# Two dense feed-forwards: one product of 512 columns in place of two of 256

## The chip, the cores and the metric

The kernel runs on one core of one Trainium2 chip, in one launch, and works on one sequence of 256 tokens with 1024 features. The metric is the device time of a run in microseconds, lower is better. All matrix products are made on TensorE (PE) in a 32-bit format (fp32r) that rounds its operands; the other engines are VectorE (DVE), ScalarE (ACT), GpSimd (POOL) and SyncE (SP), which issues the weight transfers.

## What is computed

The reference is a network of three blocks on the same 256 tokens. Layer 0 has a mixer and a dense feed-forward of width 2816. Layer 1 has another mixer and a mixture of 8 experts of width 3584, of which each token uses 2. A second block has an attention with a convolution beside it, a dense feed-forward of width 2816 and a last norm. The dense feed-forward is this:

```python
def _swiglu(x, w1, w3, w2):
    return (jax.nn.silu(x @ w1) * (x @ w3)) @ w2

# second block, on u = rms_norm(h, ...)
h = h + (jax.nn.silu(u @ w_gate[l]) * (u @ w_up[l])) @ w_down[l]
```

## The kernel before

**Three products for one.** To keep float32 precision, each operand is split into a high part (rounded to fp32r, made by ACT) and a low part (the rest, made by DVE by a subtraction); `mm3` then makes high x high, high x low and low x high and adds all three into one PSUM bank. The low x low product is left out everywhere.

**The weight stream.** All weights lie in memory as blocks of 128 x 2048 floats (1 MB each). `Stream._load` issues their transfers on SP's queue in the order of use, each into a free raw buffer; `_split` makes `wh` on ACT (L102) and `wl` on DVE (L103), each into a free split buffer. A transfer starts when a raw buffer is free, a split when its block has landed and a split buffer has been read to its end by PE. During the experts the raw buffers are those of three pools and one slot more, of the tag `b8` of the pool `xp`; 12 in all.

**A dense feed-forward** (`ffn`) runs over 11 pieces of 256 columns of width. For each it takes one block of w1, one of w3 and one of w2. `proj_cols` makes one projection, transposed: for 2 halves `ct` of 128 columns and 8 pieces `k` of the features, three matmuls of 256 columns (the tokens) with a weight of 128 x 128 each, so 48 matmuls, into the two halves of one PSUM bank. ACT takes Silu of the first projection out of PSUM (L383), DVE multiplies it by the second, still in PSUM (L385), and `parts` splits the product into `ah` and `al`. `out_mms` then makes the product with w2 in matmuls of 512 columns, one piece behind. The first piece (`proj_tok`) is made in another way and is not touched. The first feed-forward stands at about 180 to 367 us of the span, the second at about 1653 to 1835 us.

**Pools and aliases.** The pool `xp` has 6 slots of 8 KB a partition under the tag `b8`. They hold in turn the two parts of the transposed activations (`xTh`, `xTl`), those of a mixer's output (`oTh`, `oTl`), the blocks' outputs (`xn`), and during the experts `xh`, `xl`, `y`, `gy` and one raw weight buffer. Which tile gets which slot follows from the order of allocation and release. A tile that takes a slot waits until the last reader of the tile before has ended.

**The order.** A scheduler of the framework sets, when the program is built, the order in which each engine runs its instructions; each engine then runs strictly in that order and waits where data or a slot is not free. Whatever changes in pools or instructions can so move instructions elsewhere in the program.

**Three places away from the feed-forwards that the prediction speaks of.**

- The start of layer 1 (about 370 to 385 us). The layer norm's output is transposed on PE in groups of 4 (`ptr`, two groups for each 128 tokens: the features 0 to 511, and 512 to 1023) and split into `xTh` and `xTl`; then `proj_tok` multiplies (`pt`). A small weight `w_f`, loaded on POOL's queue, is split on ACT as well (`wfh`).
- The end of layer 1's mixer (about 496 to 528 us): its last products with the output weights read `oTh` and `oTl` (`acc`), then a layer norm for each 128 tokens `tt` (r = input + acc on DVE, L349; a square on ACT, L354, which uses `xn` as scratch; the reciprocal root on POOL; two scalings on DVE, L358 and L359, into `xn`), the router and the first gather for the experts.
- The collection (about 1395 to 1440 us), while the last expert runs: four indirect transfers on POOL's queue fetch rows of the other experts' outputs into the two halves of `gy`, and after each DVE adds them to `y` (L1040). A transfer into a half waits until the addition before it has read that half.

Of the kernel before, what the change touches and what calls it, by code (L numbers as in the profile page):

```python
# [10 lines left out]
F32 = mybir.dt.float32  # L11
F32R = mybir.dt.float32r
# [3 lines left out]
AF = mybir.ActivationFunctionType  # L16
ALU = mybir.AluOpType
AX = mybir.AxisListType

P = 128  # L20
D = 1024
T = 256
# [120 lines left out]
def tile_model(ctx, tc, io, out):  # L143
    nc = tc.nc
    cp = ctx.enter_context(tc.tile_pool(name="cp", bufs=1))
    xp = ctx.enter_context(tc.tile_pool(name="xp", bufs=6))
    rawp = ctx.enter_context(tc.tile_pool(name="rawp", bufs=R_RAW))
    wp = ctx.enter_context(tc.tile_pool(name="wp", bufs=N_SPLIT))
    sp = ctx.enter_context(tc.tile_pool(name="sp", bufs=4))
# [24 lines left out]
    NW = len(moe_order)  # L174
# [4 lines left out]
    ws = Stream(tc, rawp, wp, order, native=[second + i for i in NATIVE2])  # L179
# [5 lines left out]
    def bank(group, name):  # L185

        i = groups[group][turns[group] % len(groups[group])]
        turns[group] += 1
        return ps.tile([P, 512], F32, tag="bank%d" % i, name=name)

    def mmt(name="mm"):
        return bank("mm", name)

    def mm(o, l, r, start, stop):
        nc.tensor.matmul(o, l, r, start=start, stop=stop, skip_group_check=True)  # L195

    def mm3(o, lh, ll, rh, rl, start, stop):
        mm(o, lh, rh, start, False)
        mm(o, lh, rl, False, False)
        mm(o, ll, rh, False, stop)  # L200

    def split_to(oh, ol, src):
        high = nc.scalar.activation(oh, src, AF.Copy)  # L203
        return high, nc.vector.tensor_tensor(ol, src, oh.bitcast(F32), op=ALU.subtract)  # L204

    def tok(tt):
        return slice(tt * P, (tt + 1) * P)
# [50 lines left out]
        return split if full is None else copy_first  # L258

    def new_xT():  # L260
        h = xp.tile([P, 8, T], F32R, tag="b8", name="xTh")
        l = xp.tile([P, 8, T], F32R, tag="b8", name="xTl")
        return h, l

    def new_oT():
        h = xp.tile([P, 8, T], F32R, tag="b8", name="oTh")
# [3 lines left out]
    def take8():  # L270
        return [w if w is None else w.rearrange("p (k n) -> p k n", k=8) for w in ws.take()]

    def take2():
        return [w.rearrange("p (k n) -> p k n", k=2) for w in ws.take()]

    def proj_cols(xT, full=None, group="mm"):

        wh, wl = take8()
        o = bank(group, "pc")
        for ct in range(2):  # L280
            for k in range(8):
                oc = o[:, ct * 256:(ct + 1) * 256]
                if wl is None:
                    mm(oc, wh[:, k, tok(ct)], full[:, k, :], k == 0, k == 7)
                else:
                    mm3(oc, wh[:, k, tok(ct)], wl[:, k, tok(ct)], xT[0][:, k, :], xT[1][:, k, :], k == 0, k == 7)
        return o.rearrange("p (c t) -> p c t", c=2)

    def proj_tok(xT, n=1, group="mm"):

        w_ = [take8() for _ in range(n)]
        o_ = [bank(group, "pt") for _ in range(n)]
        for tt in range(2):
            for (wh, wl), o in zip(w_, o_):
                for k in range(8):
                    mm3(o[:, tt * 256:(tt + 1) * 256], xT[0][:, k, tok(tt)], xT[1][:, k, tok(tt)],
                        wh[:, k, :], wl[:, k, :], k == 0, k == 7)
        o_ = [o.rearrange("p (c t) -> p c t", c=2) for o in o_]
        return o_ if n > 1 else o_[0]
# [18 lines left out]
    def out_mms(acc, oT, w, k0, tt, first, last):  # L318

        for nh in range(2):  # L320
            for kk in range(2):
                mm3(acc[nh], oT[0][:, k0 + kk, tok(tt)], oT[1][:, k0 + kk, tok(tt)],
                    w[0][:, kk, half(nh)], w[1][:, kk, half(nh)], first and kk == 0, last and kk == 1)

    def new_acc(t):
        return [bank("acc%d" % t, "acc%d" % nh) for nh in range(2)]
# [47 lines left out]
    def ffn(fp, fr, fw, xT, n, finish):  # L374

        accs = [new_acc(0), new_acc(1)]
        ws.more(3 * n, (fr, "wraw", 4), late=True)
        ws.wider(3 * n, fw, 1, True)
        ws.first = False

        def gate(shape, h1, h3):
            s1 = fp.tile(shape, F32, tag="s1", name="s1")
            nc.scalar.activation(s1, h1, AF.Silu)  # L383
            a = fp.tile(shape, F32, tag="a", name="a")
            nc.vector.tensor_tensor(a, s1, h3, op=ALU.mult)  # L385
            return a

        def parts(a):
            ah = fp.tile([P, 2, T], F32R, tag="ah", name="ah")
            al = fp.tile([P, 2, T], F32R, tag="al", name="al")  # L390
            split_to(ah, al, a)
            return ah, al


        a = gate([P, 2, 256], *proj_tok(xT, 2))
        for j in range(1, n):
            h1 = proj_cols(xT)
            if j == 1:
                pt = mmt("pa")
                for ft in range(2):  # L400
                    for tt in range(2):
                        nc.tensor.transpose(pt[:, tok(ft * 2 + tt)], a[:, tt, tok(ft)], ident)
                aT = parts(pt.rearrange("p (f t) -> p f t", f=2))
            nxt = parts(gate([P, 2, T], h1, proj_cols(xT)))
            w = take2()
            if j < n - 1:
                for tt in range(2):
                    out_mms(accs[tt], aT, w, 0, tt, j == 1, False)
                aT = nxt
        w1 = take2()  # L410
        for tt in range(2):
            out_mms(accs[tt], aT, w, 0, tt, False, False)
            out_mms(accs[tt], nxt, w1, 0, tt, False, True)
            finish(tt, accs[tt])
# [128 lines left out]
    mrow = cp.tile([P, 1], F32, tag="mrow", name="mrow")  # L543
    nc.gpsimd.memset(mrow, -1.0 / D)
    xT = new_xT()
    for tt in range(2):
        transpose_tile(x[:, tt], "mm", parts_of(xT, tt))
# [7 lines left out]
    with tc.tile_pool(name="l0", bufs=1) as lp:  # L555
# [9 lines left out]
        with tc.tile_pool(name="gla", bufs=1) as gp:  # L565
# [12 lines left out]

            ws.first = True
            misc = proj_cols(xT)  # L580
            kiT = gp.tile([P, T], F32, tag="kiT", name="kiT")
            nc.scalar.activation(kiT, misc[:, 0, :], AF.Copy)
# [5 lines left out]
            for i in range(2):  # L588
                o = proj_cols(xT)
# [11 lines left out]
            for tt in range(2):  # L601
# [3 lines left out]
                for q in range(2):  # L605
# [5 lines left out]
                    for j in range(2):  # L611
                        rl = g2([P, 2, 256], "rl")
                        nc.scalar.activation(rl[:, :, :S], pis[j][:, :, :S], AF.Relu)
                        for i in range(2):
                            h = (2 * q + i) * 2 + j
# [33 lines left out]
            AT, xl = [], []  # L649
            for tt in range(2):  # L650
# [13 lines left out]
                for lv in range(7):  # L664
                    h = 64 >> lv
# [36 lines left out]
            for tt in range(2):  # L702
                po = bank("acc", "pog")
                for h in range(4):
                    a = 2 * (h % 2) + h // 2
# [22 lines left out]
        with tc.tile_pool(name="t0", bufs=1) as tp, tc.tile_pool(name="t0w", bufs=2) as wo:  # L728
# [25 lines left out]
            xT = xT2  # L754
# [3 lines left out]
    with tc.tile_pool(name="f0", bufs=2) as fp, tc.tile_pool(name="f0r", bufs=4) as fr, tc.tile_pool(name="f0w", bufs=1) as fw:  # L758
# [13 lines left out]
        x, xT = xn, xT2  # L772
# [62 lines left out]
    with tc.tile_pool(name="l1", bufs=1) as lp:  # L835
# [75 lines left out]
        with tc.tile_pool(name="t1", bufs=1) as tp, tc.tile_pool(name="t1w", bufs=1) as wo:  # L911
# [27 lines left out]
            def finish(tt, acc):  # L939
                if tt == 1:  # L940
                    transpose_tile(xn[:, 0], "acc0", router(0))
                normed.extend(residual_ln(tp, x, acc, lnp, xn, tt, router(1) if tt else None, 1))
# [22 lines left out]
    with tc.tile_pool(name="moer", bufs=4) as mr, tc.tile_pool(name="moe2", bufs=2) as m2:  # L965
        ws.first = False
        ws.more(NW, (mr, "wraw", 4))
        ws.more(NW, (xp, "b8", 1), late=True)
        xh = xp.tile([P, 2, D], F32R, tag="b8", name="xh")
        xl_ = xp.tile([P, 2, D], F32R, tag="b8", name="xl")  # L970
        y = xp.tile([P, 2, D], F32, tag="b8", name="y")
        for tt in range(2):
            with tc.issue_after((copied[-1] if tt else normed[-2]).ins):
# [59 lines left out]

        def collect():

            gy = xp.tile([P, 2, D], F32, tag="b8", name="gy")
            for tt in range(2):
                for k in range(2):
                    nc.gpsimd.indirect_dma_start(gy[:, k], None, yg_d, bass.IndirectOffsetOnAxis(ap=rg[:, tt, k:k + 1], axis=0))
                    nc.vector.scalar_tensor_tensor(y[:, tt], gy[:, k], gk[:, tt, k:k + 1], y[:, tt], op0=ALU.mult, op1=ALU.add)  # L1040
# [130 lines left out]
        xT = new_xT()  # L1171
# [25 lines left out]
    with tc.tile_pool(name="s1", bufs=1) as lp:  # L1197
# [15 lines left out]
        for ct in range(4):  # L1213
            o = proj_cols(xT, xTf)
# [27 lines left out]
        with tc.tile_pool(name="t2", bufs=1) as tp, tc.tile_pool(name="t2w", bufs=1) as wo:  # L1242
# [3 lines left out]
            xT = new_xT()  # L1246
# [40 lines left out]
    with tc.tile_pool(name="f2", bufs=2) as fp, tc.tile_pool(name="f2r", bufs=4) as fr, tc.tile_pool(name="f2w", bufs=1) as fw:  # L1287
        fing = bcast(fp, io["fin_g"], "fing")

        o = xp.tile([P, 2, D], F32, tag="b8", name="o")  # L1290
# [130 lines left out]
def build(arrays):  # L1421
    import concourse.bacc as _bacc

    nc = _bacc.Bacc("TRN2", target_bir_lowering=False, num_devices=1)
    io = {n: nc.dram_tensor("in_" + n + "_dram", a.shape, mybir.dt.from_np(a.dtype), kind="ExternalInput").ap()
          for n, a in arrays.items()}
    out = nc.dram_tensor("out_0_dram", (T, D), F32, kind="ExternalOutput").ap()
    with tile.TileContext(nc) as tc:
        tile_model(tc, io, out)
    return nc  # L1430
# [9 lines left out]
```

## Time and profile before

| | |
|---|---|
| median of 3 runs | 1846.14 us (1843.38 to 1847.57) |
| the profiled execution, device time | 1845.33 us |
| its span, first to last instruction | 1843.5 us |
| mean granted TensorE clock | 0.982 of full speed |
| PE, DVE, ACT, POOL busy | 97%, 73%, 59%, 5% of the span |
| weight blocks split (wh, wl) | 446 each |
| read from memory | 495.57 MB |

The span leaves out about 1.8 us of the device time at the launch's ends. Busy PE is the share of time in which a matmul was under way; matmuls overlap, so that a busy PE need not be at its peak.

### The profile page before, as it was taken

How to read it: one execution, taken by the hardware profiler on the slowest of the kernel's cores; microseconds unless marked ns; L12 is line 12 of the kernel's file. 1: busy time of each engine (PE TensorE's matmuls, PEld its weight loads, DVE VectorE, ACT ScalarE, POOL GpSimd, SP SyncE). 2: the span in 40 equal slices, each digit the busy share in tenths (PEclk: the TensorE clock that was granted, in tenths of full speed). 3: DMA queues.
4: the chain of work that ended last, by engine and by line, in shares of the span. 5: the costliest groups of instructions: out<-in, count | busy, mean ns of one | idle time of the engine just before them, and what ended most of it. 6: DMA issues, size and time to landing. Idle time of an engine off the chain costs nothing. (4 is left out here: it accounts for less than half of the span.)

```text
span 1843.5 us, 24483 instructions
## 1 busy us (share of the span) xinstructions
PE 1782.0 (97%) x9857; PEld 1512.4 (82%) x9857; DVE 1338.1 (73%) x1363; ACT 1096.1 (59%) x1016; POOL 83.9 (5%) x133
## 2 busy tenths in 40 slices
PE   8999999999999999999999999999998987999998
PEld 7887999888778888888788787887886867889997
DVE  6866544545678888888888888888887877955443
ACT  5454433344567777777777777777775754564442
POOL 1101100010010000000000000000002002000000
PEclk9999999999989999999999999999999998999999
DMA  8442985254379999999999999999998933546530
GB/s 297 161 163 103 390 329 186 89 196 158 117 300 423 381 371 371 382 355 366 374 367 368 381 364 375 371 368 373 366 364 321 361 139 140 206 155 250 190 125 24
DMA packets 75418, 512.50 MB, mean 278 GB/s; under 512 B 8572, under 2 KB 8725, under 8 KB 17312
## 3 DMA queue, kind: packets, MB, share of 16 engines
q1 hardware_dynamic: 66096, 475.62, 68.2%
q0 software_dynamic: 8912, 34.70, 5.0%
q8 instruction: 80, 1.31, 0.3%
q10 hardware_dynamic: 288, 0.52, 0.1%
q14 instruction: 42, 0.34, 0.0%
HBM read 495.57 MB, written 19.96 MB: 280 GB/s over the span
## 5 line engine op out<-in xcount | busy, mean ns | idle before, releaser
L103 DVE TENSOR_TENSOR wl<-wraw,wh 128x2048 fp32r<-128x2048 f32 (+1 forms) x446 | 1011.3, 2284 | 306.6 <-ACT wh L102 304.8
L102 ACT ACTIVATE wh<-wraw 128x2048 fp32r<-128x2048 f32 (+1 forms) x446 | 851.8, 1912 | 465.5 <-issue 133.3
L195 PE MATMUL hh<-wl,eTh 128*128 128x512 f32 x896 | 356.0, 397 | 5.2 <-DVE wl L103 5.2
L195 PE MATMUL hh<-wh,eTh 128*128 128x512 f32 x896 | 355.6, 397 | 0.0
L195 PE MATMUL hh<-wh,eTl 128*128 128x512 f32 x896 | 353.5, 395 | 0.0
L195 PE MATMUL pc<-xTh,wh 128*128 128x256 f32 x944 | 270.8, 287 | 1.0 <-ACT xTh L203 1.0
L195 PE MATMUL pc<-xTl,wh 128*128 128x256 f32 x944 | 269.7, 286 | 0.8 <-DVE xTl L204 0.8
L195 PE MATMUL pc<-xTh,wl 128*128 128x256 f32 x944 | 269.6, 286 | 0.0
L195 PEld LDWEIGHTS hh<-wl,eTh 128*128 128x128 f32 x896 | 169.3, 189 | 47.8 <-DVE wl L103 9.5
L195 PEld LDWEIGHTS hh<-wh,eTh 128*128 128x128 f32 x896 | 169.1, 189 | 38.9 <-ACT eTh L203 0.2
L195 PEld LDWEIGHTS hh<-wh,eTl 128*128 128x128 f32 x896 | 169.0, 189 | 38.2
L195 PE MATMUL acc<-wl,mah 128*128 128x512 f32 x448 | 181.7, 406 | 5.9 <-DVE wl L103 5.9
L195 PEld LDWEIGHTS pc<-xTh,wh 128*128 128x128 f32 x944 | 183.2, 194 | 4.0 <-ACT xTh L203 1.4
L195 PEld LDWEIGHTS pc<-xTl,wh 128*128 128x128 f32 x944 | 183.1, 194 | 2.0 <-DVE xTl L204 1.3
L195 PEld LDWEIGHTS pc<-xTh,wl 128*128 128x128 f32 x944 | 183.3, 194 | 0.2 <-issue 0.2
L195 PE MATMUL acc<-wh,mal 128*128 128x512 f32 x448 | 177.6, 397 | 0.3 <-DVE mal L204 0.3
L195 PE MATMUL acc<-wh,mah 128*128 128x512 f32 x448 | 164.2, 396 | 0.5 <-ACT mah L203 0.5
L195 PEld LDWEIGHTS acc<-wl,mah 128*128 128x128 f32 x448 | 85.0, 190 | 24.2 <-DVE wl L103 6.4
L195 PEld LDWEIGHTS acc<-wh,mah 128*128 128x128 f32 x448 | 84.7, 189 | 20.7 <-ACT mah L203 0.9
L195 PEld LDWEIGHTS acc<-wh,mal 128*128 128x128 f32 x448 | 85.2, 190 | 18.5 <-DVE mal L204 0.8
L195 PE MATMUL pt<-wh,xTh 128*128 128x256 f32 x256 | 74.2, 291 | 0.5 <-ACT xTh L203 0.4
L195 PE MATMUL pt<-wl,xTh 128*128 128x256 f32 x256 | 73.6, 288 | 0.2 <-DVE wl L103 0.2
(332 smaller groups left out, 1851.8 us busy)
## 6 DMA issues: line engine op xcount, KB each, us to landing
wraw<-in_w_m_dram SPq DMA_DIRECT2D x336, 1024.0 KB, 7.3
wraw<-in_w_d_dram SPq DMA_DIRECT2D x33, 1024.0 KB, 5.7
wraw<-in_w_dram SPq DMA_DIRECT2D x33, 1024.0 KB, 4.9
wraw<-in_w_ab_dram SPq DMA_DIRECT2D x14, 1024.0 KB, 4.9
wraw<-in_w_cd_dram SPq DMA_DIRECT2D x12, 1024.0 KB, 4.9
wraw<-in_w_in_dram SPq DMA_DIRECT2D x10, 1024.0 KB, 4.9
xg_d<-zero POOLq DMA_DIRECT2D x8, 1024.0 KB, 43.8
rows<-scr POOLq DMA_DIRECT2D x3, 1536.0 KB, 11.6
```

The lines of the kernel that those rows point to most:

```text
L102: nc.scalar.activation(wh[:, c], raw[:, c], AF.Copy)
L103: nc.vector.tensor_tensor(wl[:, c], raw[:, c], wh[:, c].bitcast(F32), op=ALU.subtract)
L195: nc.tensor.matmul(o, l, r, start=start, stop=stop, skip_group_check=True)
```

## The change

- A new `proj_wide` stands in for `proj_cols` in both feed-forwards (10 pieces with two projections each, so 40 blocks of weights). For each `ct` and `k` it makes one matmul of the high weight with both parts of x at once, 512 columns, which fills a whole bank, and one of 256 columns of the low weight with the high part of x, into the bank's first half. A projection so takes two banks, one for each `ct`, and its two halves have to be added.
- `added` does this: for each `ct` ACT copies the second half of the bank to SBUF and DVE adds the first half to it. Silu and the multiplication then read and write these SBUF tiles.
- For one product of 512 columns the two parts of x have to lie beside each other. They are now one tile of 16 KB, in a pool of its own with one buffer (`xtp`); the experts' `xh` and `xl` (now `xhl`) and `gy` use the same buffer later. For this `xp` goes from 6 slots to 4, and the experts lose the raw buffer that stood there (11 in place of 12).

```diff
-    xp = ctx.enter_context(tc.tile_pool(name="xp", bufs=6))
+    xp = ctx.enter_context(tc.tile_pool(name="xp", bufs=4))
+    xtp = ctx.enter_context(tc.tile_pool(name="xtp", bufs=1))
...
     def new_xT():
-        h = xp.tile([P, 8, T], F32R, tag="b8", name="xTh")
-        l = xp.tile([P, 8, T], F32R, tag="b8", name="xTl")
-        return h, l
+        both = xtp.tile([P, 8, 2, T], F32R, tag="xT", name="xT")
+        return both[:, :, 0], both[:, :, 1], both
...
+    def proj_wide(xT):
+        wh, wl = take8()
+        o = [mmt("pc") for _ in range(2)]
+        for ct in range(2):
+            for k in range(8):
+                mm(o[ct], wh[:, k, tok(ct)], xT[2][:, k], k == 0, False)
+                mm(o[ct][:, :T], wl[:, k, tok(ct)], xT[0][:, k, :], False, k == 7)
+        return o
...
+        def added(o, name):
+            t = fp.tile([P, 2, T], F32, tag=name, name=name)
+            for ct in range(2):
+                nc.scalar.activation(t[:, ct], o[ct][:, T:], AF.Copy)
+                nc.vector.tensor_tensor(t[:, ct], t[:, ct], o[ct][:, :T], op=ALU.add)
+            return t
...
         for j in range(1, n):
-            h1 = proj_cols(xT)
+            h1 = added(proj_wide(xT), "s1")
...
-            nxt = parts(gate([P, 2, T], h1, proj_cols(xT)))
+            h3 = added(proj_wide(xT), "a")
+            nxt = parts(gate(h1, h3, h1, h3))
...
-        ws.more(NW, (xp, "b8", 1), late=True)
-        xh = xp.tile([P, 2, D], F32R, tag="b8", name="xh")
-        xl_ = xp.tile([P, 2, D], F32R, tag="b8", name="xl")
+        xhl = xtp.tile([P, 2, 2, D], F32R, tag="xT", name="xhl")
+        xh, xl_ = xhl[:, 0], xhl[:, 1]
...
-            gy = xp.tile([P, 2, D], F32, tag="b8", name="gy")
+            gy = xtp.tile([P, 2, D], F32, tag="xT", name="gy")
```

The lines of the kernel after are 1 to 21 higher than before in what follows (L203 becomes L204, L354 becomes L366, L930 becomes L951, L1040 becomes L1060, L1132 becomes L1152).

**Place 1, the start of layer 1.** This is ACT's order there, before. The four copies `xTh<-ptr` are, in this order, features 0 to 511 and 512 to 1023 of the first 128 tokens (3514, 3521) and the same of the second 128 (3568, 3575):

```order
L354 ACTIVATE xn_1882,ss_3558<-r_3552,nmu_3556 128x1024
L203 ACTIVATE xTh_1883<-ptr_3514 128x4x128
L203 ACTIVATE xTh_1883<-ptr_3521 128x4x128
L203 ACTIVATE xTh_1883<-ptr_3568 128x4x128
L203 ACTIVATE wfh_3632<-w_f_3630 128x64
L203 ACTIVATE xTh_1883<-ptr_3575 128x4x128
L102 ACTIVATE wh_3654<-wraw_3409 128x2048
```

And this is ACT's order there in the changed kernel, where 3294 and 3301 are the two groups of the first 128 tokens, 3348 and 3355 those of the second:

```order
L366 ACTIVATE xn_1883,ss_3338<-r_3332,nmu_3336 128x1024
L204 ACTIVATE xT_1884<-ptr_3294 128x4x128
L204 ACTIVATE xT_1884<-ptr_3348 128x4x128
L204 ACTIVATE wfh_3412<-w_f_3410 128x64
L204 ACTIVATE xT_1884<-ptr_3301 128x4x128
L204 ACTIVATE xT_1884<-ptr_3355 128x4x128
L102 ACTIVATE wh_3434<-wraw_3201 128x2048
```

The split of `w_f` now stands ahead of two copies, among them the second group of the first tokens, and no longer ahead of the last copy alone.

**Place 2, the end of layer 1's mixer.** ACT's order before; `xn_4634` is the layer's output, `wh` are splits of expert weights, `xTf` copies for the router, and the brackets name the engines waited for:

```order
L354 ACTIVATE xn_4634,ss_4906<-r_4900,nmu_4904 128x1024 [waits DVE_49]
L203 ACTIVATE oTh_3616<-po_4930 128x2x128 [waits PE_49]
L102 ACTIVATE wh_4746<-wraw_4303 128x2048 [waits DMAHW0_49,PE_49]
L102 ACTIVATE wh_4813<-wraw_4412 128x2048 [waits DMAHW2_49,PE_49]
L930 ACTIVATE xTf_4997<-ptr_4992 128x512 [waits PE_49,Activation_49]
L930 ACTIVATE xTf_5008<-ptr_5003 128x512 [waits PE_49,Activation_49]
L354 ACTIVATE xn_4634,ss_5046<-r_5040,nmu_5044 128x1024 [waits DVE_49]
```

ACT's order there in the changed kernel, where the layer's output is `xn_4414`:

```order
L204 ACTIVATE oTh_3396<-po_4710 128x2x128 [waits PE_49]
L102 ACTIVATE wh_4526<-wraw_4083 128x2048 [waits DMAHW0_49,PE_49]
L102 ACTIVATE wh_4593<-wraw_4192 128x2048 [waits DMAHW2_49,PE_49]
L366 ACTIVATE xn_4414,ss_4686<-r_4680,nmu_4684 128x1024 [waits DVE_49,PE_49]
L951 ACTIVATE xTf_4777<-ptr_4772 128x512 [waits PE_49,Activation_49]
L951 ACTIVATE xTf_4788<-ptr_4783 128x512 [waits PE_49,Activation_49]
L366 ACTIVATE xn_4414,ss_4826<-r_4820,nmu_4824 128x1024 [waits DVE_49]
```

The square of the first 128 tokens moved behind the copy and both splits, and has got a wait for PE: `xn_4414` now takes the slot of `oTl_3397`, which the last products of the mixer read. On DVE its two scalings into `xn` moved behind two splits in the same way.

**Place 3, the collection.** DVE's order before; `ms1` is the gate's multiplication of one expert piece, `y` the additions of fetched rows, `wl` splits of expert weights:

```order
L103 TENSOR_TENSOR wl_11499<-wraw_11245,wh_11498 128x2048
L1132 TENSOR_TENSOR ms1_11495<-ms1_11495,hh_11497 128x512
L1040 SCALAR_TENSOR_TENSOR y_5088<-gy_11440,gk_3598,y_5088 128x1024
L103 TENSOR_TENSOR wl_11517<-wraw_11263,wh_11516 128x2048
L1040 SCALAR_TENSOR_TENSOR y_5088<-gy_11440,gk_3598,y_5088 128x1024
L103 TENSOR_TENSOR wl_11538<-wraw_11282,wh_11537 128x2048
L1040 SCALAR_TENSOR_TENSOR y_5088<-gy_11440,gk_3598,y_5088 128x1024
L103 TENSOR_TENSOR wl_11556<-wraw_11300,wh_11555 128x2048
L1040 SCALAR_TENSOR_TENSOR y_5088<-gy_11440,gk_3598,y_5088 128x1024
L103 TENSOR_TENSOR wl_11575<-wraw_11319,wh_11574 128x2048
```

DVE's order there in the changed kernel, from the last split ahead of the additions:

```order
L103 TENSOR_TENSOR wl_11246<-wraw_11022,wh_11245 128x2048
L1060 SCALAR_TENSOR_TENSOR y_4867<-gy_11217,gk_3378,y_4867 128x1024
L103 TENSOR_TENSOR wl_11276<-wraw_11040,wh_11275 128x2048
L1060 SCALAR_TENSOR_TENSOR y_4867<-gy_11217,gk_3378,y_4867 128x1024
L103 TENSOR_TENSOR wl_11294<-wraw_11059,wh_11293 128x2048
L1060 SCALAR_TENSOR_TENSOR y_4867<-gy_11217,gk_3378,y_4867 128x1024
L1152 TENSOR_TENSOR ms1_11272<-ms1_11272,hh_11274 128x512
L1060 SCALAR_TENSOR_TENSOR y_4867<-gy_11217,gk_3378,y_4867 128x1024
L103 TENSOR_TENSOR wl_11315<-wraw_11077,wh_11314 128x2048
L103 TENSOR_TENSOR wl_11333<-wraw_11096,wh_11332 128x2048
```

The first addition stands one split earlier in the stream of weights: the split that was the last ahead of it is now the first behind it. Between the third and the fourth addition a gate stands in place of a split, and that gate was ahead of all four before.

## Rows read from the trace of the kernel before

**Rows 1.** Windows: busy us of each engine, then PEclk, DMA share, GB/s.
```profile
193.00:355.00 162.00, 162.00 (x1159) 153.37 (x1158) 79.66 (x50) 65.34 (x49) 4.06 (x6) 1.00 0.66 250
385.00:495.00 110.00, 109.90 (x812) 94.39 (x811) 60.05 (x169) 57.79 (x117) 1.08 (x2) 0.98 0.46 160
600.00:1400.00 800.00, 796.78 (x3551) 645.86 (x3550) 687.37 (x383) 586.80 (x397) 7.33 (x14) 1.00 0.96 370
```
**Rows 2.** The chain that ended last, one piece of the second feed-forward: start, us, what.
```profile
1676.20 11.51 PE pc L195 x96
1687.71 5.47 PE acc L195 x24
```
**Rows 3.** The costliest groups of the page: busy us, mean ns of one, idle before.
```profile
L195 PE MATMUL pc<-xTh,wh 128*128 128x256 f32 x944 | 270.8, 287 | 1.0 <-ACT xTh L203 1.0
```
**Rows 4.** Copies and subtractions, by tile (min/median/max ns) and in the first feed-forward.
```profile
L203 ACT ACTIVATE oTh<-po x16: 362/384/387, 144.8 to 1628.3; 128x256 fp32r<-128x256 f32 x16
...
L204 DVE TENSOR_TENSOR oTl<-po,oTh x16: 401/418/425, 146.7 to 1628.7; 128x256 fp32r<-128x256 f32 x16
...
L204 DVE TENSOR_TENSOR al<-a,ah 128x512 fp32r<-128x512 f32 x10 | 6.8, 684 | 0.0
```
**Rows 5.** Timeline at the start of layer 1: start us, us, what, idle before.
```profile
375.45 0.54 POOL L217 DMA_DIRECT2D w_f<-in_w_f_dram  x1
...
382.64 0.26 ACT L203 ACTIVATE wfh<-w_f 128x64 fp32r<-128x64 f32 x1 [6.69 <-DMA w_f<-in_w_f_dram]
382.80 0.58 ACT L203 ACTIVATE xTh<-ptr 128x512 fp32r<-128x512 f32 x1
...
376.18 0.41 PE L195 MATMUL pt<-wh,xTh 128*128 128x256 f32 x1
...
378.52 0.33 PE L195 MATMUL pt<-wh,xTl 128*128 128x256 f32 x1
```
**Rows 6.** Windows at the start of layer 1 and in the collection.
```profile
378.50:384.00 5.50, 5.50 (x48) 5.50 (x46) 0.58 (x1) 0.74 (x2) 0.00 (x0) 0.99 0.99 404
...
1414.00:1419.00 5.00, 5.00 (x12) 3.95 (x13) 3.47 (x2) 0.80 (x2) 3.46 (x2) 0.50 0.80 297
```
**Rows 7.** Timeline at the end of layer 1's mixer.
```profile
497.21 1.15 ACT L354 ACTIVATE xn<-r,nmu 128x1024 f32<-128x1024 f32 x1
...
510.95 1.15 ACT L354 ACTIVATE xn<-r,nmu 128x1024 f32<-128x1024 f32 x1
...
500.36 1.42 DVE L359 SCALAR_TENSOR_TENSOR xn<-r,rs_b,lnb 128x512 f32<-128x512 f32 x2 [0.46 <-POOL rs_b L336]
...
509.48 0.69 DVE L349 SCALAR_TENSOR_TENSOR r<-xn,acc 128x512 f32<-128x512 f32 x1 [0.67 <-PE acc L195]
...
509.05 0.40 PE L195 MATMUL acc<-wh,oTl 128*128 128x512 f32 x1
...
515.99 1.51 PE L239 MATMUL ptr<-ident,xn 128*128 128x128 f32 x6 [2.11 <-DVE xn L359]
```
**Rows 8.** Timeline of the collection.
```profile
1400.78 2.29 DVE L103 TENSOR_TENSOR wl<-wraw,wh 128x2048 fp32r<-128x2048 f32 x1 [0.34 <-ACT wh L102]
...
1410.42 1.28 DVE L1040 SCALAR_TENSOR_TENSOR y<-gy,gk,y 128x1024 f32<-128x1024 f32 x1 [5.79 <-DMA gy<-yg_d,rg]
...
1413.98 1.28 DVE L1040 SCALAR_TENSOR_TENSOR y<-gy,gk,y 128x1024 f32<-128x1024 f32 x1
...
1420.08 1.28 DVE L1040 SCALAR_TENSOR_TENSOR y<-gy,gk,y 128x1024 f32<-128x1024 f32 x1 [2.61 <-DMA gy<-yg_d,rg]
...
1423.49 1.28 DVE L1040 SCALAR_TENSOR_TENSOR y<-gy,gk,y 128x1024 f32<-128x1024 f32 x1
...
1413.95 0.80 PE L195 MATMUL acc<-wl,mah 128*128 128x512 f32 x1 [5.92 <-DVE wl L103]
...
1432.24 0.39 PE L195 MATMUL hh<-wh,eTl 128*128 128x512 f32 x1
```
**Rows 9.** What the experts' engines waited for, 600 to 1400 us: us in total, times, longest.
```profile
ACT wh L102 <- PE hh L195: 83.1, 132, 1.0
```

More of the change, by code (lines that the diff above doesn't have):

```diff
@@ L379, in ffn, with gate @@
         ws.first = False
-        def gate(shape, h1, h3):
-            s1 = fp.tile(shape, F32, tag="s1", name="s1")
+        def gate(h1, h3, s1=None, a=None):
+            s1 = s1 or fp.tile([P, 2, 256], F32, tag="s1", name="s1")
             nc.scalar.activation(s1, h1, AF.Silu)
-            a = fp.tile(shape, F32, tag="a", name="a")
+            a = a or fp.tile([P, 2, 256], F32, tag="a", name="a")
             nc.vector.tensor_tensor(a, s1, h3, op=ALU.mult)
@@ L392, in parts @@
             return ah, al
-        a = gate([P, 2, 256], *proj_tok(xT, 2))
+        def added(o, name):
[4 more added lines that the diff above has]
+            return t
+        a = gate(*proj_tok(xT, 2))
         for j in range(1, n):
-            h1 = proj_cols(xT)
+            h1 = added(proj_wide(xT), "s1")
             if j == 1:
```

## The prediction

> **What bounds the kernel now.** I read the busy windows first. In the first feed-forward PE is busy for all of 162.00 us at a granted clock of 1.00, while DVE is busy for 79.66 and ACT for 65.34; PE is full again through layer 1 from 385 us on (109.90 of 110.00), and through the experts (796.78 of 800) [rows 1]. So a microsecond that PE saves in the feed-forward is saved at the end, and a microsecond for which PE stands still later is lost: no later stretch before the experts has slack to take it back, and in the experts, though the DMA engines are busy for 0.96, what ACT's splits wait for is PE (83.1 us in 132 waits) [rows 1, 9].
>
> Second, the chain that ended last gives the true price of a matmul. Two projections are 96 matmuls of 256 columns in 11.51 us, 119.9 ns each; 24 matmuls of 512 columns with w2 take 5.47 us, 228 ns each [rows 2]. The page's table shows 287 ns for one of 256 [rows 3], but that is from start to modelled end, of matmuls that overlap, and is not used. The Trainium skill says the same (Trainium Kernel Development and Optimization, Performance Expectations: matmul busy time is a bad metric because matmuls are pipelined); the trace agrees, 287 beside 119.9.
>
> Third, since pools change, I compared the order of instructions, and read at the three places shown above what PE waits for there, in timelines [rows 5, 7, 8].
>
> **The change, part by part.**
>
> *The product.* Each block loses 32 matmuls of 256 columns (239.8 ns a pair) for 16 of 512 columns (228 ns): 11.9 ns saved a pair, 16 x 11.9 = 0.19 us a block, 40 blocks: 7.6 us. The bounds: nothing, if a long product followed by a short one has a longer pitch than either alone; or 17 us, if it went at 512 columns / 2.4 GHz = 213 ns, with nothing around it (26.5 x 640). I take 7.6, since rows 2 have this very form of matmul, with a weight of its own each.
>
> A rule speaks against even that. The Trainium skill (TensorE: Matmul & The Clock Gate, Back-to-back issue gap) gives N / 2.4 + 2.5 ns for a lone stream: joining two would then save 2.5 ns a pair, by my estimate from it 1.6 us in all, and the forecast below would be 6 us later. The trace has 119.9 ns where this gives 109.2, so here more hangs on each matmul than the rule allows.
>
> *The evacuation.* Four copies on ACT (384 ns each) and four additions on DVE (418 ns each) [rows 4] come to each piece of 16.98 us: 1.5 us on ACT, 1.7 us on DVE. They are hidden: both engines are busy for half a piece or less [rows 1], the two halves are split over two banks so that the first is emptied while PE fills the second, and the result is read one piece later. If that cover were gone, 20 pieces would cost up to 3.2 us each. It is gone only in the last piece of each feed-forward, where PE multiplies the result at once, after 24 matmuls of the piece before (5.47 us). In the first, ACT and DVE have a weight split between copy and parts; the low part (684 ns, rows 4) comes within some tenths of 5.47 us. Bounds 0 and 1.5 us, I take 0.5.
>
> *The start of layer 1.* The split of `w_f` waits for a transfer that POOL issues at 375.45; it runs at 382.64, the copy behind it at 382.80 for 0.58 us [rows 5]. Before, this copy is needed last, about 84 matmuls after 376.18, and PE had work all the while: 11 matmuls in 2.34 us to 378.52 at 0.213 us each, then the fast pitch, 48 matmuls recorded in 5.50 us at clock 0.99 [rows 5, 6]. After, features 512 to 1023 of the first tokens stand behind `wfh` too, so PE has only the 10 matmuls left of features 0 to 511: 376.2 + 10 x 0.213 = 378.3, then nothing until 382.80 + 0.58 = 383.4. It stands for 5.1 us. What is late next is the clock: PE restarts cold. At the lower clock 12 matmuls of 512 columns took 5.00 us (clock 0.50) [rows 6] where the fast pitch is 2.7, so 1 (the excess of the 11 above: 11 x 0.093) to 2.3 us. Together 6.1 to 7.4 us, and nothing if `w_f` landed by 378; POOL's order is row by row the same and its transfers hang on the same layer norm, so I take 6.
>
> *The end of layer 1's mixer.* The square of the first tokens ran at 497.21, under the products of the second, and the scalings into `xn` ended at 500.36 + 1.42 = 501.78: 4.6 us in all [rows 7]. After, it must wait for the last product that reads the slot, 509.05 + 0.40, so `xn` is done at 514.0. The two residual additions of the second tokens (0.69 each) stand behind it on DVE, so their square starts at about 515.5, where it started at 510.95 [rows 7]: 4.5 us. The router, the gather and the first expert hang on it, by way of the transposes (515.99 before). Some of the small router steps fill the new gap, so 3.5 to 4.5; I take 4. Nothing, if `xn` didn't need the slot at once; the order shows that it does.
>
> *The collection.* DVE stands still for 5.79 us for the first fetched rows (addition at 1410.42), and again for the third (1420.08) [rows 8]. Each split queued behind an addition is late for PE. Before, the split that ran at 1400.78 came in time, the next one after 1410.42 + 1.28 let PE go on at 1413.95 after 5.92 us [rows 8]. After, the split of 1400.78 itself stands behind the first addition, and PE stops at the product before, some 12 matmuls sooner. The second split comes after 1413.98, and the third only after the third addition, the gate, and the fourth (1423.49): 1423.49 + 1.28 + 2.29 = 1427.1. Then PE has 47 matmuls of the experts' first product before it, at 228 ns 10.7 us: 1437.8, where it ended at 1432.24 + 0.39 = 1432.6. That is 5.2 us, and up to 7.5 with a second cold start (2.3). It could be nothing if the fetches, issued off the same additions, landed sooner. I take 5.5.
>
> *The experts.* A raw buffer fewer of 12 is hidden while splits wait for PE and not for data [rows 9]. Both ways: 0, or a stall of a few microseconds early on, when the buffers are filled; I take 0.
>
> **The sum.** -7.6 + 0.5 + 6 + 4 + 5.5 = +8.4 us on the profiled execution's 1845.3 (span 1843.5 and 1.8 around it): 1853.7. The median is 0.8 higher than that execution; I forecast 1853.5. The bound for faster and slower is 0.2%, 3.7 us, about what a measurement of this kernel can tell from no change.
>
> **The rivals.**
>
> *One or two of the three stalls don't come* (the collection's most likely, since it hangs on when fetched rows land; or `w_f` lands early). Without the collection 1848.2, without layer 1's start 1847.7, without both 1842.2. For it: these stalls are put together from the order, and one wait hidden behind another counts once. Against: the places are 100 us and more apart, with PE full between them. Chance 0.20, no change.
>
> *All three are covered, only the product counts.* 1845.3 - 7.6 = 1837.7, faster. It decides if the order of engines matters less than it looks, for instance if DVE came to each place with microseconds to spare. Against: PE is seen waiting at two of the three already [rows 7, 8]. Chance 0.07.
>
> *The long product costs no more than a short one*, because a weight load and not the columns sets the pitch of both. Then 640 x 119.9 = 76.7 us go, against 16 us of stalls: 1784.6, faster. For it: the pitch of 119.9 is longer than 256 columns at 2.4 GHz (106.7). Against: 228 ns for 512 columns in rows 2. The Trainium skill has such a price (the same page and section: about 131 ns a matmul of 512 columns in a real stream with weight loads), by which 70 us would go; the trace has 228 and doesn't agree. Chance 0.03.
>
> *The experts starve*, or the evacuation doesn't fit: slower than 1858. Every 3 us lost on top needs one block to come late by that much; decided by whether splits wait for transfers after about 545 us. Chance 0.08.
>
> **How the numbers follow.** My forecast has 0.62 and its own range is 1850 to 1858 (product between -10 and -4, layer 1's start 4 to 7.4, the mixer's end 3.5 to 4.5, the collection 3 to 7.5). With the rival of one stall missing (0.20, at 1847.7 and 1848.2, less when part of another goes too) the range is 1845 to 1858, and leaves out 0.18 (0.10 faster, 0.08 above). Faster 0.11 (0.07 + 0.03 and the case of two missing stalls and a cheaper product), same 0.20, slower 0.69.
>
> **What would show it.** Right: in the changed profile 32 short and 32 long matmuls of a piece's two projections at some 11.1 us in place of 11.51; PE idle for `xT` behind `wfh` at the start of layer 1 for about 5 us; the square of the first tokens starting after the last `acc` and the transposes of the second about 4 us later against it; PE waiting for two `wl` around the additions, in place of one long wait. Wrong: a pitch of the long product far from 228 ns; `w_f` landing before PE asks; PE's stand in the collection unchanged; or a new wait of PE inside the feed-forwards or the experts, that I do not see in the order.

## The result and the profile after

| | before | after |
|---|---|---|
| median | 1846.14 us (1842.67 to 1851.88, 7 runs) | 1858.58 us (1856.36 to 1861.51, 7 runs) |
| ratio to before | | 1.0075, 95% interval 1.0059 to 1.009 |
| the profiled execution | 1845.33 us | 1859.15 us |
| its span | 1843.5 us | 1857.4 us |
| mean granted TensorE clock | 0.982 | 0.977 |
| matmuls | 9857 | 9217 |

The kernel became slower, as forecast, by 12.4 us where 7.4 (8.4 against the profiled execution) was forecast; the time lies 0.6 us above the range's end of 1858.

**Where the time went.** All 446 weight blocks are split in the same order in both kernels, so the start of the n-th `wh` of ACT (counted from 0) is the same point of the work in both timelines. The difference of these starts, after less before, is a ledger:

```
wh no.  before    after    difference   between this row and the next
  24    189.14   187.76     -1.38       first feed-forward:          -1.15
  55    367.52   364.99     -2.53       start of layer 1:            +6.47
  56    385.71   389.65     +3.94       rest of layer 1:             -1.47
  70    503.95   506.42     +2.47       end of its mixer, gather:    +5.15
  72    532.01   539.62     +7.62       experts up to the fetches:   +0.84
 372   1401.14  1409.60     +8.46       collection:                  +6.86
 384   1447.07  1462.38    +15.32       second block to its ffn:     +0.19
 417   1656.30  1671.81    +15.51       second feed-forward:         -1.36
 445   1812.13  1826.28    +14.15       (end of the span: +13.8)
```

The three places named in the prediction carry +18.5, the two feed-forwards -2.5. The -1.38 before the first feed-forward and the -1.47 in layer 1 lie where executions of the same instructions differ by as much and more: the run e4 below has the instructions of the changed kernel up to the collection and is at +1.5 in the rest of layer 1, with a granted clock of 0.97 there, where the changed kernel has 1.00 and the kernel before 0.99. Without the two the stages sum to +16.7 at the end of the span, while the medians differ by 12.4 (the interval of the ratio is 10.9 to 16.6 us); how much of the rest is chance, one profile of each kernel can't tell.

**The product.** This is the chain that ended last in the changed kernel, one piece of the second feed-forward (start, us, what), which answers to [rows 2]:

```profile
1691.60 11.29 PE pc L196 x64
1702.89 5.50 PE acc L196 x24
```

Two projections now take 11.29 us in place of 11.51: 0.22 us saved a piece, where 0.38 was forecast. The product with w2 behind them takes 5.50 in place of 5.47, so that a whole piece saves 0.19. The timeline of PE in the same piece shows the alternation, a long product, a short one, a long one:

```profile
1692.49 0.40 PE L196 MATMUL pc<-xT,wh 128*128 128x512 f32 x1
1692.72 0.28 PE L196 MATMUL pc<-xT,wl 128*128 128x256 f32 x1
1692.84 0.40 PE L196 MATMUL pc<-xT,wh 128*128 128x512 f32 x1
```

The long one starts 0.23 us before the short one and the short one 0.12 before the next long one. Over the whole piece the medians of these steps are 236 and 118 ns, where 228 and 120 had been taken. From 191 to 366 us of the changed kernel, its first feed-forward, PE waits once, in the last piece, for the split of the gated product:

```profile
PE acc L196 <- ACT ah L204: 0.5, 1, 0.5
```

**Layer 1's start.** The timeline of the changed kernel, first ACT, then PE (answers to [rows 5]):

```profile
372.91 0.60 ACT L204 ACTIVATE xT<-ptr 128x512 fp32r<-128x512 f32 x1 [4.30 <-PE ptr L240]
379.88 0.26 ACT L204 ACTIVATE wfh<-w_f 128x64 fp32r<-128x64 f32 x1 [6.38 <-DMA w_f<-in_w_f_dram]
380.05 1.06 ACT L204 ACTIVATE xT<-ptr 128x512 fp32r<-128x512 f32 x2
...
376.29 0.41 PE L196 MATMUL pt<-wh,xT 128*128 128x256 f32 x1
380.68 0.58 PE L196 MATMUL pt<-wh,xT 128*128 128x256 f32 x1 [3.97 <-ACT xT L204]
```

Both copies behind `wfh` run at 380.05, and PE stands for 3.97 us until the first of them is done. This is the window behind that stand, in the form of [rows 1]:

```profile
380.60:384.00 3.40, 3.32 (x14) 3.10 (x15) 1.62 (x4) 0.51 (x2) 0.00 (x0) 0.51 1.01 390
```

The granted clock is 0.51, nearly all of it the lower level of 1.2 GHz, where the kernel before had 0.99 from 378.5 on [rows 6]; a matmul steps by 0.21 us in place of 0.12. Over these 3.3 us that loses about 1.4 more (an estimate from the two steps). The stand and the slow restart come to some 5.4 of the 6.5 us; the run e2 below shows the same share, and what the rest is.

**The mixer's end** (answers to [rows 7]). ACT, PE and DVE in the changed kernel:

```profile
511.94 1.15 ACT L366 ACTIVATE xn<-r,nmu 128x1024 f32<-128x1024 f32 x1 [3.61 <-PE acc L196]
...
518.14 1.15 ACT L366 ACTIVATE xn<-r,nmu 128x1024 f32<-128x1024 f32 x1 [0.22 <-DVE nmu L364]
...
511.52 0.39 PE L196 MATMUL acc<-wh,oTl 128*128 128x512 f32 x1
516.00 1.23 PE L240 MATMUL ptr<-ident,xn 128*128 128x128 f32 x8 [4.09 <-DVE xn L371]
524.16 1.94 PE L240 MATMUL ptr<-ident,xn 128*128 128x128 f32 x8 [1.91 <-DVE xn L371]
...
516.55 0.69 DVE L361 SCALAR_TENSOR_TENSOR r<-xn,acc 128x512 f32<-128x512 f32 x1
```

The square starts when the last product that reads `oTl` has ended (511.52 + 0.39), PE waits 4.09 us for the scaled `xn`, and the second square starts 6.2 us behind the last product, where it was 1.5 in [rows 7].

**The collection** (answers to [rows 8]). DVE, then the waits of PE:

```profile
1417.94 1.28 DVE L1060 SCALAR_TENSOR_TENSOR y<-gy,gk,y 128x1024 f32<-128x1024 f32 x1 [9.04 <-DMA gy<-yg_d,rg]
1419.14 2.28 DVE L103 TENSOR_TENSOR wl<-wraw,wh 128x2048 fp32r<-128x2048 f32 x1
1421.34 1.28 DVE L1060 SCALAR_TENSOR_TENSOR y<-gy,gk,y 128x1024 f32<-128x1024 f32 x1
1422.54 2.28 DVE L103 TENSOR_TENSOR wl<-wraw,wh 128x2048 fp32r<-128x2048 f32 x1
1427.65 1.28 DVE L1060 SCALAR_TENSOR_TENSOR y<-gy,gk,y 128x1024 f32<-128x1024 f32 x1 [2.83 <-DMA gy<-yg_d,rg]
1428.85 0.68 DVE L1152 TENSOR_TENSOR ms<-ms,hh 128x512 f32<-128x512 f32 x1
1431.47 1.28 DVE L1060 SCALAR_TENSOR_TENSOR y<-gy,gk,y 128x1024 f32<-128x1024 f32 x1 [1.94 <-DMA gy<-yg_d,rg]
...
1421.48 0.80 PE L196 MATMUL acc<-wl,mah 128*128 128x512 f32 x1 [8.65 <-DVE wl L103]
1435.01 0.80 PE L196 MATMUL hh<-wl,eTh 128*128 128x512 f32 x1 [4.55 <-DVE wl L103]
```

PE's one long wait of 5.92 us [rows 8] became two, of 8.65 and 4.55, each for a split that stood behind an addition. The fourth addition waits as well (1.94), which I had not counted.

### The profile page after: what moved, and what is told of

It is laid out like the page before. It is cut to its first block, busy times and chain, and to the rows that moved or that the text cites. A ratio compares the mean times of both kernels' runs of the same rounds, so it can differ in the third digit from the quotient of the medians.

```text
span 1857.4 us, 23370 instructions
## 1 busy us (share of the span) xinstructions
PE 1779.7 (96%) x9217; PEld 1478.1 (80%) x9217; DVE 1366.0 (74%) x1443; ACT 1125.1 (61%) x1096; POOL 80.9 (4%) x133
## 5 line engine op out<-in xcount | busy, mean ns | idle before, releaser
L196 PE MATMUL pc<-xT,wh 128*128 128x512 f32 (+1 forms) x1248 | 341.1, 345 | 2.8 <-ACT xT L204 1.5
L196 PE MATMUL pc<-xT,wl 128*128 128x256 f32 x944 | 267.0, 283 | 0.0
L196 PEld LDWEIGHTS pc<-xT,wh 128*128 128x128 f32 x1248 | 216.8, 191 | 35.2 <-DVE xT L205 1.9
L196 PEld LDWEIGHTS pc<-xT,wl 128*128 128x128 f32 x944 | 180.1, 191 | 1.1 <-issue 0.2
L196 PE MATMUL pt<-wh,xT 128*128 128x256 f32 x512 | 99.9, 294 | 5.4 <-ACT xT L204 4.8
L196 PEld LDWEIGHTS pt<-wh,xT 128*128 128x128 f32 x512 | 84.0, 199 | 8.5 <-ACT xT L204 5.8
L196 PE MATMUL pt<-wl,xT 128*128 128x256 f32 x256 | 74.3, 291 | 0.0
L196 PE MATMUL acc<-wh,ah 128*128 128x512 f32 x176 | 69.2, 393 | 0.5 <-ACT ah L204 0.5
```

## The experiments

Each is read in two ways: by its median against runs of the kernel before on the same chip, and by the same ledger in its profile. This is the ledger of all of them, in us against the profile of before, by the stages above ("start" is all before the first feed-forward):

```
                  start   ffn 1  layer-1  rest of  mixer's  experts collec-  second   ffn 2
                                 start    layer 1  end              tion     block
after              -1.4    -1.2    +6.5    -1.5    +5.1    +0.8    +6.9    +0.2    -1.4
e1 pools only      -3.1    +0.0    +0.1    +0.0    +5.6    +1.0    +7.2    +0.2    +0.0
e2 w_f behind      +0.8    -1.2    +0.9    -0.0    +5.6    +1.0    +6.5    +0.6    -1.4
e3 xn free slot    -4.7    -1.2    +6.2    -1.5    -0.7    +0.9    +6.2    +0.4    -1.3
e4 four places     -2.0    -1.2    +5.9    +1.5    +5.7    +1.0    -0.9    +1.6    -1.3
e5 grouped         -5.0    -3.4    -2.0    -2.0    +5.1    +0.9    +6.3    +0.5    -3.1
e6 before, late    -0.8    +0.0    +0.1    +0.0    +0.0    +0.1   -10.6    +2.1    +0.0
e7 all, late       -5.2    -1.2    +1.1    -1.5    -0.3    +0.8   -10.6    +3.9    -1.3
e8 all, grouped    -2.2    -3.4    -2.0    +1.4    -0.7    +0.9   -10.6    +1.1    -3.1
```

The places are read from the ledger, since one place is near the noise of the medians. Each against its own before, the medians stand at +12.4 for the changed kernel and at +9.5, +10.6 and +8.7 for e2, e3 and e4, with intervals of some 3 us to either side. So taking away one wait gave 2.9, 1.8 and 3.7 us by the medians, and 5.6, 5.9 and 7.8 at its place in the ledger. What the medians do show clear of noise is all three taken away, in e7.

My theory at this point was that three displaced waits cost some 18 us and the product gives back 2 to 4; the rivals were that the evacuation, or the loss of a raw buffer, or crowded transfers cost it.

**e1: the pools alone.** The change with the old projections.

```diff
-            h1 = added(proj_wide(xT), "s1")
+            h1 = proj_cols(xT)
...
-            h3 = added(proj_wide(xT), "a")
-            nxt = parts(gate(h1, h3, h1, h3))
+            nxt = parts(gate(h1, proj_cols(xT)))
```

> The pools and aliases of the change, with the old projections (three matmuls of 256 columns, no evacuation to SBUF). The order shows that the split of w_f stands as in the kernel before, while the square of the first tokens and the additions of the collection stand as in the changed kernel. If the loss comes from displaced waits, the mixer's end (+5.2 us), the collection (+6.9) and a small shift early in the experts (+0.9) stay and the product's gain and the stall of layer 1's start are gone: 1859 us. If instead the evacuation of the wide product costs the time and the pools are harmless, it runs like the kernel before, 1846 us.

Measured: 1855.62 us, ratio 1.0063 (1.0047 to 1.008), 11.9 above before, which itself ran at 1843.75 beside it, 2.4 lower than beside the changed kernel. The mixer's end and the collection stay (+5.6, +7.2), layer 1's start and the feed-forwards are as before. So two of the three stalls come from the pools alone. The third comes only with the new product: with other instructions in the feed-forward the scheduler put `wfh` at another place. The evacuation is not what costs, since without it and without the wide product most of the loss is there.

**e2: `w_f` behind the copies.** The split of `w_f` is queued behind the last copy of `xT`.

```diff
-            transpose_tile(xn[:, tt], "acc%d" % tt, use)
+            turned.append(transpose_tile(xn[:, tt], "acc%d" % tt, use))
...
-            split_to(wfh, wfl, wfr)
+            with tc.issue_after(turned[-1][0].ins), tc.issue_after(turned[-1][1].ins):
+                split_to(wfh, wfl, wfr)
```

> The changed kernel with the split of w_f queued behind all four copies of xT. If PE stood for the copies behind that split, the 6.5 us at layer 1's start come back: 1852 us. If the stand is only moved to the forget gate that needs w_f, or to the next block of weights, the time stays at 1858.6 us.

Measured: 1853.27 us, ratio 1.0052 (1.0035 to 1.0069). In its ledger +6.5 became +0.9, so 5.6 of the 6.5 us were this wait. The 0.9 that stays is PE's transposes behind the second tokens' layer norm: four of the first tokens' have moved behind that wait, so that 12 run there in place of 8 (first the kernel before, then e2):

```profile
374.20 1.97 PE L239 MATMUL ptr<-ident,xn 128*128 128x128 f32 x8 [1.41 <-DVE xn L359]
...
373.94 2.82 PE L240 MATMUL ptr<-ident,xn 128*128 128x128 f32 x12 [1.41 <-DVE xn L373]
```

ACT's timeline there shows that the split now waits without harm, all copies being ahead of it:

```profile
376.80 0.60 ACT L204 ACTIVATE xT<-ptr 128x512 fp32r<-128x512 f32 x1 [0.26 <-PE ptr L240]
380.25 0.26 ACT L204 ACTIVATE wfh<-w_f 128x64 fp32r<-128x64 f32 x1 [2.85 <-DMA w_f<-in_w_f_dram]
386.23 1.92 ACT L102 ACTIVATE wh<-wraw 128x2048 fp32r<-128x2048 f32 x1 [5.72 <-PE pt L196]
```

**e3: a free slot for `xn`.** One early raw weight buffer had taken the slot that `xn` could have had; both `b8` raw buffers now come with the experts.

```diff
-            ws.more(4 + NW, (xp, "b8", 2))
...
         ws.more(NW, (mr, "wraw", 4))
+        ws.more(NW, (xp, "b8", 2), late=True)
```

> The changed kernel, with the two raw buffers under the tag b8 given to the weight stream only at the experts' start, so that xn finds a free slot before the mixer ends. If the wait of the square for the last reader of oTl is the cause, 5 us come back at the mixer's end: 1853.5 us. If the experts start on the weights that were loaded into these slots early, they wait for transfers instead: 1858 us or more.

Measured: 1854.38 us, ratio 1.0056 (1.0041 to 1.0072). The mixer's end went from +5.1 to -0.7, and the experts did not start later on their weights. ACT's timeline has the square ahead of the last `oTh` again:

```profile
496.10 1.15 ACT L366 ACTIVATE xn<-r,nmu 128x1024 f32<-128x1024 f32 x1
...
497.85 0.39 ACT L204 ACTIVATE oTh<-po 128x256 fp32r<-128x256 f32 x1 [0.51 <-PE po L196]
```

Against its own before the median fell by less than the ledger, 1.8 where 5.9 went at this place, which is within the noise of the two medians.

**e4: four places for the fetched rows.** They fill the 16 KB slot; the additions stand behind the gates of the second to fifth piece of the last expert.

```diff
-            gy = xtp.tile([P, 2, D], F32, tag="xT", name="gy")
+            gy = xtp.tile([P, 4, D], F32, tag="xT", name="gy")
...
-                    nc.vector.tensor_tensor(s1, s1, h3, op=ALU.mult)
+                    mul = nc.vector.tensor_tensor(s1, s1, h3, op=ALU.mult)
+                    if later and 1 <= j <= 4:
+                        with tc.issue_after(mul.ins):
+                            later[0](j - 1)
```

> The changed kernel, with four places for the fetched rows (they fill the 16 KB of the slot), so that the four fetches don't wait for the additions, and each addition queued behind the gate of one of the next four pieces. If PE stood for splits that are queued behind additions waiting for rows, both the 6.9 us added by the change and most of the 11 us lost there before come back: 1841 us. If PE stands because the fetches crowd the weight transfers out, the stand stays: 1855 to 1859 us.

Measured: 1852.47 us, ratio 1.0046 (1.003 to 1.0062): 11.5 us above the expected time. The addition of the change is gone (+6.9 became -0.9), but the stand of the kernel before is not. This is DVE around the first addition, and POOL's four issues:

```profile
1414.84 0.69 DVE L1155 TENSOR_TENSOR ms<-ms,hh 128x512 f32<-128x512 f32 x1 [0.86 <-PE hh L196]
1422.69 1.29 DVE L1062 SCALAR_TENSOR_TENSOR y<-gy,gk,y 128x1024 f32<-128x1024 f32 x1 [7.16 <-DMA gy<-yg_d,rg]
1423.89 2.28 DVE L103 TENSOR_TENSOR wl<-wraw,wh 128x2048 fp32r<-128x2048 f32 x1
...
1412.96 1.91 POOL L1058 DMA_INDIRECT gy<-yg_d,rg  x1 [7.63 <-DMA yg_d<-oe]
1417.69 0.94 POOL L1058 DMA_INDIRECT gy<-yg_d,rg  x1 [0.30 <-issue]
```

The first gate comes 1.9 us after the first fetch is issued, and the row 9.7 us after it: the addition was not late enough. This left the rival open that transfers crowd each other; e6 decides it.

**e5: long and short products grouped.**

```diff
             for k in range(8):
                 mm(o[ct], wh[:, k, tok(ct)], xT[2][:, k], k == 0, False)
+            for k in range(8):
                 mm(o[ct][:, :T], wl[:, k, tok(ct)], xT[0][:, k, :], False, k == 7)
```

> The changed kernel with the 16 products of a half put in another order: first the 8 of 512 columns, then the 8 of 256, into the same bank. In the changed kernel, where they alternate, the start of a long one and of the next short one lie 236 ns apart, 9 more than between two long ones of the product with w2 (227). If the alternation costs this, each feed-forward becomes shorter by 320 x 9 = 2.9 us; if the wide product itself costs 236 ns, neither changes. In both cases the order at layer 1's start happens to fall as in the kernel before (the split of w_f behind all copies), which gives back 6.5 us. So 1845 us by the first, 1851 by the second, where the kernel before has 1844 to 1846.

Measured: 1845.85 us, ratio 1.0017 (1.0002 to 1.0031). The chain has the piece at 11.15 us (11.29 alternating, 11.51 before):

```profile
1676.54 11.15 PE pc L196 x64
```

The feed-forwards went from -1.2 and -1.4 to -3.4 and -3.1, together 4.0 more where 5.8 was expected. So the alternation does cost: 0.14 us in a piece of 32 pairs, and 0.03 in the product with w2, which is back at 5.47 (the chain of e8 below), some 5 ns a pair in all. In a piece of e8 the medians of long after long and short after short are 228 and 120 ns, the price that the prediction took from [rows 2]. Layer 1's start is 2.0 ahead of before, as the order there changed once more: the first tokens' copy now stands ahead of the second tokens' square. That the time is the 1845 expected is luck: the feed-forwards gave back 1.8 less than expected and layer 1's start 2 more.

**e6: the kernel before with late additions.** As e4, with two `b8` tiles, and the gates of the third to sixth piece (`2 <= j <= 5`).

> The kernel before, with nothing changed but the collection: four places for the fetched rows, and the additions queued behind the gates of the third to sixth piece of the last expert, later than in the run with four places, where the first addition still waited 7.2 us for its row. If the additions' wait is the whole of PE's stand there, it takes 11 us off the kernel before: 1834 us. If fetches and weights crowd each other on the DMA engines, a stand of several us stays: 1840 us or more.

Measured: 1834.7 us, ratio 0.9946 (0.9926 to 0.9966), 8.9 us below before. In the collection 10.6 us are gone, and DVE finds its row there when it comes to the first addition:

```profile
1420.93 0.69 DVE L1135 TENSOR_TENSOR ms<-ms,hh 128x512 f32<-128x512 f32 x1 [0.86 <-PE hh L195]
1421.53 1.28 DVE L1042 SCALAR_TENSOR_TENSOR y<-gy,gk,y 128x1024 f32<-128x1024 f32 x1
```

Three of the four additions now stand behind the collection's last row of the ledger and cost 0.5 us each there, which is 1.5 of the +2.1 of the second block; so some 9 us are won in all, as by the median. All four fetches are issued within 6 us here, closer together than before, and the stand is gone: it was that of splits behind waiting additions, and not one of crowded transfers. For the changed kernel e7 shows the same, with the same -10.6.

**e7: the change with all three waits taken away** (e2, e3, and e4 with `2 <= j <= 5`).

> The changed kernel with all three waits taken away: w_f split behind the copies of xT, a free slot for xn, four places for the fetched rows with their additions behind the third to sixth gate. If those three waits and a product worth 3.5 us explain the change, this is 11 + 3.5 us faster than the kernel before, less about 1 us early in the experts: 1831 to 1833 us, and 2 to 3 us faster than the kernel before with late additions. If the change costs time in another way as well, it isn't faster than that one.

Measured: 1833.44 us, ratio 0.9944 (0.9925 to 0.9963). That is 1.3 us less than e6, which the spread of runs doesn't tell from none. The change is not clean of side effects here: the ledger has 2.5 us won in the feed-forwards, and against it 1.0 more than e6 at layer 1's start and 0.8 in the experts. So even without the three waits the change with the alternating product is worth next to nothing: these two losses take most of what the product gains.

**e8: the same with grouped products.**

> The same with the products grouped by length. 5.8 us less than the one with all three waits taken away if the alternation of lengths costs 9 ns a pair, 1826 us; the same time if the wide product has this price by itself.

Measured: 1828.33 us, ratio 0.9915 (0.9894 to 0.9936), the fastest of all: 15.2 us below before and 5.1 below e7, where 5.8 was expected. Not all of the 5.1 is the grouping: the ledger has 4.0 more in the feed-forwards, and 3.2 at layer 1's start, whose order is that of e5, less what the clock took back elsewhere (0.97 in the rest of layer 1, where e7 has 1.00). Its chain, the same piece:

```profile
1654.94 5.47 PE acc L196 x24
1660.41 11.15 PE pc L196 x64
```

## Why the prediction was wrong

*The product.* Forecast 7.6 us (228 against 239.8 ns a pair); measured 3.8 by the chain (0.19 x 20 pieces), and 2.5 in the ledger, where the last pieces' loss is taken off. The step that failed is the one that took the long product's price from a row in which long ones follow long ones. Here each follows a short one and precedes one, and costs 236. Grouped, by nothing but the order, a long one costs 228, and the chain saves 0.36 a piece (16.98 less 11.15 and 5.47), 7.2 us in all (6.5 in the ledger): the price was right for a form that the change didn't have. The lower bound, "nothing, if a long product followed by a short one has a longer pitch", had the mechanism, and I put the value at the other end. The rule of the Trainium skill (TensorE: Matmul & The Clock Gate, Back-to-back issue gap), by which 2.5 ns a pair is saved, is too low for the trace in both forms: 6.9 ns alternating (0.22 us over 32 pairs), 11 grouped (0.36 over 32). The other price of that section, 131 ns for a long product, is shown by no run here: none is below 223.

*The evacuation.* Right that it hides: in the first feed-forward PE waits for it once, in the last piece, for 0.5 us, and in the second not at all. In the last piece of the first the ledger loses 0.7 us (from -3.21 at split 54 to -2.53 at 55), where 0.5 was forecast for both.

*Layer 1's start.* Right in place and size, 6.5 against 6; PE stood for 3.97 us, the restart at the lower clock cost about 1.4, and 0.9 came from four transposes that moved behind a wait, which I had not counted. I had the stand at 5.1 us and 1 to 2.3 for the clock, 6.1 to 7.4 together, so that the 6 taken lay below its own bounds.

*The mixer's end.* Right in place; 5.15 against 4. I took off half a microsecond for router steps that would fill the gap. In the trace they come later too (the first of them on DVE at 520.99 in place of 512.62), since their own input hangs on the first `xn`, and the second scaling stands behind them as before.

*The collection.* Right in place; 6.9 against 5.5. The step that failed counted two waits of DVE, for the first and the third fetch. The fourth fetch, issued behind the second addition, is waited for as well (1.94 us); it was hidden before, by the split that stood ahead of it.

*The experts.* Taken at 0, measured +0.8 to +1.0 in each run with the smaller `xp`, e1 and e7 included. One wait of PE for a split accounts for most of it:

```profile
794.04 0.50 PE L196 MATMUL hh<-wl,eTh 128*128 128x512 f32 x1 [0.62 <-DVE wl L103]
```

Both kernels have such a wait at the end of each later expert (the kernel before 0.64 at 907.53 first); in the changed kernel they begin one expert earlier. Which of the changed slots does this was not tried.

*The sum.* All these misses point the same way: by the ledger the terms come to some 17 us where 8.4 were summed, by the medians to 12.4. Two steps of the sum made it worse. From 1853.7 and a median 0.8 above the profiled execution it should have gone to 1854.5, and it went to 1853.5. And the range ended at 1858, though the highest values named for it, with 0.5 for the evacuation, come to +15.9, which is 1861. The rivals: all three stalls came, in full; nothing was covered by a later stretch, as PE's full windows had said. The long product did not cost as little as a short one, and the experts did not starve.

## What to carry to other kernels

Read the price of a matmul from rows in which it stands among the same neighbours: here a long one costs 236 ns between short ones and 228 between long ones, and by the chain grouping them gave almost as much again as the merging. A change of pools is judged by what the slots and the order do elsewhere: list what takes each slot, and what stands behind each wait on each engine, since two of three stalls came without the product. An instruction that waits for a transfer should stand in an engine's queue where the row has long landed: four places for the rows and later additions took 9 us off the kernel before.

## What was not expected of the hardware

The same instructions take several microseconds more or less in different executions, though PE is busy in all of them. The runs e2 and e3 differ only from layer 1 on, yet e3 starts its first feed-forward 5.5 us earlier. PE's waits between 25 and 110 us are the same in both, 4.2 us in all with 1.4 the longest. Their windows from 30 to 100 us, e2 first:

```profile
30.00:100.00 70.00, 65.74 (x511) 58.16 (x510) 56.35 (x146) 32.51 (x39) 7.01 (x6) 0.93 0.46 162
```

```profile
30.00:100.00 70.00, 65.75 (x549) 59.10 (x548) 55.60 (x145) 33.64 (x40) 7.00 (x6) 1.00 0.45 163
```

PE is busy for 65.7 us in both, but at a granted clock of 0.93 it gets through 511 matmuls and at 1.00 through 549. Most of the 5.5 us is made there. Single runs of the kernel before spread by more than that (1842.67 to 1851.88), and the longer ones have the lower mean clock: of the 17 runs beside e5 to e8 the fastest has 1838.26 us at 0.987 and the slowest 1849.06 at 0.980. In which stretch they lose it is not shown for these. What decides whether the clock stays up in this stretch was not tried.
